# Stick-breaking attention: softplus, its parts and the log two steps ahead of the running total, scores three, and every second rounding on ScalarE

## The chip, the core and the metric

The kernel runs on one core of a Trainium2 chip. The core has five engines, each with its own instruction queue, worked off in order: TensorE (PE in the rows, PEld for its weight loads), VectorE (DVE), ScalarE (ACT), GpSimd (POOL) and SyncE (SP, which only starts transfers). The metric is the device time of one launch in microseconds (us). A difference under 0.3% (4.85 us of 1615.97) can't be told from no change.

## The reference, cut to what matters

One layer: a projection, gating and stick-breaking attention, an output projection, and a mixture of experts. The change is in the attention alone, 4 heads over 1024 positions:

```
z = einsum('bhqd,bhkd->bhqk', qb, kf[:, :, :kl]) * scale
causal = arange(kl)[None, :] < q_pos[:, None]
log_fail = where(causal, log_sigmoid(-z), 0.0)            # -softplus(z)
within = einsum('bhqni,ij->bhqnj', log_fail, after_in_block)
blk = sum(log_fail, axis=-1)
later = cumsum(blk, axis=3, reverse=True) - blk
log_a = log_sigmoid(z) + (within + later[..., None])
a = where(causal, exp(log_a), 0.0)
outs.append(einsum('bhqk,bhkd->bhqd', a, vt[:, :, :kl]))
```

The sum over later keys is a running total: a key block can only be finished when all later blocks have been added.

## The kernel before, in words

Attention works on transposed tiles: 128 keys on the partitions, up to 512 queries (one half of the sequence) along the row. A `Chain` is one head of one half. Two chains, an even and an odd head, go side by side as a pair. A step is one key block of a pair, from the last block (`top`) down to block 0; the list `seq` holds all 24 steps. On the diagonal a step has fewer columns: both pairs of the first half have steps of 128, 256, 384 and 512 columns (steps 0 to 3 and 4 to 7), both of the second half 128, 256, 384 and five times 512 (steps 8 to 15 and 16 to 23).

For each chain and step: `z` makes the scores on PE (plain float32, two passes each, and a mask product on the diagonal). `e0`, `e1`, `e2` make log(1+exp(-|z|)) on ACT, in tile `e`. `sp` adds max(z,0) on DVE, which gives softplus; it is then split in two parts, `sh` (rounded to float32r, line 682) and the rest `sl` (POOL, line 683). `ls` makes log_sigmoid(z) on DVE. `tri` adds both parts into the running total `cum` in PSUM with two matmuls, `add` (DVE, line 702) adds the total to `ls`, `comp` completes the total for the next block, `exp` is on ACT and `av` multiplies with V into `yp`.

The order on every engine is the order of the program text (`manual_schedule`). The loop at line 784 goes over k; one pass is called turn k here. Turn k does `tri`, `add`, `comp` and `exp` of step k, `av` of step k-1 (for the first step of a pair one turn later), and beside them work for later steps. When a pair has ended, `fin0` to `fin5` normalise its output: fin0 in the turn after (four ACT functions), fin1 to fin3 one turn later (column sums on PE, a power on POOL at line 128, a broadcast on PE at line 736, a product on DVE at line 740), then fin4 on ACT and fin5 (tile `yl`, DVE). This happens three times inside the loop, in turns 5, 9 and 17; the last pair is finished in the next stage, the output projection, which starts with `wo` on ACT.

Tiles come from rings: z has 4 buffers, e 4, sp 2, sh 4, sl 4, ls 8, two per step.

Of the kernel before, what the change touches and what calls it, by code (L numbers as in the profile page):

```python
# [11 lines left out]
F32R = mybir.dt.float32r  # L12
I32 = mybir.dt.int32
AF = mybir.ActivationFunctionType
# [3 lines left out]
P = 128  # L18
# [40 lines left out]
def body(ctx, tc, A, out):  # L59
    nc = tc.nc  # L60
    V, G, T, SC, SY = nc.vector, nc.gpsimd, nc.tensor, nc.scalar, nc.sync
# [364 lines left out]
    def at(s, fn):  # L426
        todo.setdefault(s, []).append(fn)
# [192 lines left out]
    def wo_load(i):  # L620
        if i < 16:
            cg, b = i // 4, (i + 2) % 4
            wo_raw[i] = wr.tile([P, 2, 512], F32, name="wo")
            SY.dma_start(wo_raw[i], A["w_out"][cg, b])
# [8 lines left out]
    def ya_load(t):  # L633
        y = op.tile([P, DG], F32, name="yld")
        SY.dma_start(y, y_d[t * P:(t + 1) * P, :])
        return y

    with ExitStack() as c3:
        at_ = c3.enter_context(tc.tile_pool(name="at", bufs=4, reuse_waits="tile"))
# [3 lines left out]
        class Chain:  # L643
# [31 lines left out]
            def sp(self, j):  # L675
                z, e = self.k[j]
                q0 = self.q0(j)
                sp = at_.tile([P, 512], F32, name="sp", bufs=2)[:, q0:]
                sh = at_.tile([P, 512], F32R, name="sh")[:, q0:]
                sl = at_.tile([P, 512], F32R, name="sl")[:, q0:]  # L680
                V.scalar_tensor_tensor(sp, z, 0.0, e, op0=ALU.max, op1=ALU.add)  # L681
                V.tensor_copy(sh, sp)  # L682
                G.tensor_tensor(sl, sp, sh.bitcast(F32), op=ALU.subtract)  # L683
                self.k[j] += [sh, sl]

# [66 lines left out]
        with tc.manual_schedule():  # L752
            seq = []
            for half in range(2):
                for hp2 in range(2):
                    ch = [Chain(half, 2 * hp2), Chain(half, 2 * hp2 + 1)]
                    seq += [(ch, j) for j in range((half + 1) * HT - 1, -1, -1)]
            n = len(seq)

            def each(i, f):  # L760
                if 0 <= i < n:
                    ch, j = seq[i]
                    for c in ch:
                        f(c, j)

            for i in range(2):
                wo_load(i)
            G.dma_start(wgr, A["w_gr"])
            yas = {t: ya_load(t) for t in range(2)}

            def scores(i):
                for f in (Chain.e0, Chain.e1, Chain.e2):
                    each(i, f)

            def first(i):
                return 0 <= i < n and seq[i][1] == seq[i][0][0].top

            each(0, Chain.z)
            each(1, Chain.z)
            scores(0)  # L780
            each(0, Chain.sp)
            each(0, Chain.ls)
            scores(1)
            for k in range(n + 1):
                each(k, Chain.tri)
                each(k, Chain.add)
                each(k + 2, Chain.z)
                each(k, Chain.comp)
                if 0 < k and seq[k - 1][1] == 0:
                    for i in range(6):  # L790
                        for c in seq[k - 1][0]:
                            at(k + (0, 1, 1, 1, 2, 3)[i], getattr(c, f"fin{i}"))
                if first(k - 2):
                    each(k - 2, Chain.av)
                if not first(k - 1):
                    each(k - 1, Chain.av)
                each(k + 1, Chain.sp)
                each(k + 1, Chain.ls)
                each(k + 2, Chain.e0)
                each(k, Chain.exp)  # L800
                each(k + 2, Chain.e1)
                each(k + 2, Chain.e2)
                for f in todo.pop(k, []) if k < n else ():
                    f()
            fins = [f for k in sorted(todo) for f in todo[k]]
            todo.clear()
# [386 lines left out]
    def pool(name, bufs=1):  # L1193
        return ctx.enter_context(tc.tile_pool(name=name, bufs=bufs, reuse_waits="tile"))
# [11 lines left out]
    sl = pool("sl")  # L1206
# [313 lines left out]
```

## Time and profile before

| | |
|---|---|
| median of 3 runs | 1615.97 us (1611.76 to 1616.34) |
| the profiled execution | 1613.13 us, of which 1611.4 us span |
| mean granted TensorE clock | 0.976 |
| PE busy in the span | 1517.6 us (94%) |
| DVE, ACT, POOL busy | 1217.1, 948.1 and 311.5 us |
| attention | from 536 to 667 us of the span |

A busy share over the span hides the stage: attention is 8% of the span, and its DMA queues are nearly idle. What the change does can only be seen there, in what each engine waits for.

### The profile page before, as it was taken

Reading aid. Unit: us, or ns where it says so; the run is one execution under the profiler, and the core shown is the slowest. Engines: PE = TensorE matmul, PEld = TensorE weight load, DVE = VectorE, ACT = ScalarE, POOL = GpSimd, SP = SyncE. Lnnn points to the kernel's source line nnn. Section 1 sums busy time; section 2 is a strip of 40 time slices with the busy share of each in tenths; the row PEclk is TensorE's granted clock in tenths of the full one; section 3 lists DMA queues with packets and bytes.
Section 4 is the critical chain, followed back from the end, with each engine's and each line's share of the span. In section 5 each row is a group of like instructions: output and inputs, shape, how many; then the busy total and the mean of one; then the engine's idle time right before and its main releaser. Section 6 shows DMA issues by size and latency. Waiting matters only on the chain.

```text
span 1611.4 us, 21345 instructions
## 1 busy us (share of the span) xinstructions
PE 1517.6 (94%) x6818; PEld 1150.6 (71%) x6818; DVE 1217.1 (76%) x2220; ACT 948.1 (59%) x2016; POOL 311.5 (19%) x286
## 2 busy tenths in 40 slices
PE   4999998999999899899999869999989999999996
PEld 4788887788888666578878756666656666666664
DVE  5889675867777588768756768887868888888883
ACT  5442588755434677532223567777767777777771
POOL 2000132010011244320001222324221212211111
PEclk9899999999999999999999979999999999999998
DMA  9987477768776000468857558999999999999982
GB/s 379 357 311 250 154 257 282 258 237 315 275 271 230 1 1 1 139 225 299 291 189 281 210 211 324 349 369 346 388 341 366 359 363 369 366 362 357 357 300 33
DMA packets 94393, 433.94 MB, mean 269 GB/s; under 512 B 13072, under 2 KB 13184, under 8 KB 64192
## 3 DMA queue, kind: packets, MB, share of 16 engines
q1 hardware_dynamic: 82000, 377.54, 63.3%
q0 software_dynamic: 11984, 52.85, 11.2%
q10 hardware_dynamic: 288, 2.10, 0.3%
q8 instruction: 56, 0.92, 0.2%
q14 instruction: 65, 0.53, 0.1%
HBM read 399.89 MB, written 43.02 MB: 275 GB/s over the span
## 4 chain that ended last, share of the span: by engine, by line
PE 38%; DMA 35%; issue 14%; DVE 6%; ACT 3%; POOL 2%; POOLq 0%; SPq 0%; another core or an unknown queue 0%; DVEq 0%; ACTq 0%
DMA out<-y,idx 22%; PE acc L322 21%; PE acc L867 9%; DMA xg<-u_d,idx 7%; DMA wm<-in_w_mod 2%; DMA out<-xi 2%; DVE macc L182 1%; PE lg L913 1%; PE yp L719 1%; POOL sl L683 1%; PE z L655 1%; DVE sp L681 1%; DVE sh L682 1%; PE tr L906 1%; ACT junk L347 1%
## 5 line engine op out<-in xcount | busy, mean ns | idle before, releaser
L1282 DVE TENSOR_TENSOR wl<-wx,wh 128x1024 fp32r<-128x1024 f32 x256 | 309.6, 1219 | 13.9 <-ACT wh L1281 12.9
L1281 ACT ACTIVATE wh<-wx 128x1024 fp32r<-128x1024 f32 x256 | 273.7, 1071 | 46.5 <-PE gu L1291 36.8
L1314 PE MATMUL dn<-wx,actT 128*128 128x512 f32 x512 | 241.9, 596 | 5.8 <-DMA wx<-in_w_down 5.2
L1291 PE MATMUL gu<-wh,xh 128*128 128x512 f32 x512 | 239.9, 469 | 0.0
L182 DVE SCALAR_TENSOR_TENSOR macc<-wm,sc_c,macc 128x512 f32<-128x512 f32 x296 | 222.3, 751 | 11.4 <-DMA wm<-in_w_mod 3.3
L322 PE MATMUL acc<-wh,hh 128*128 128x512 f32 x640 | 209.9, 398 | 3.2 <-ACT hh L278 1.8
L322 PE MATMUL acc<-wl,hh 128*128 128x512 f32 x640 | 206.9, 394 | 2.8 <-DVE wl L307 2.5
L322 PE MATMUL acc<-wh,hl 128*128 128x512 f32 x640 | 205.8, 392 | 0.4 <-DVE hl L279 0.4
L1291 PE MATMUL gu<-wl,xh 128*128 128x512 f32 x512 | 203.1, 397 | 0.1
L1291 PE MATMUL gu<-wh,xl 128*128 128x512 f32 x512 | 202.0, 394 | 0.0
L1224 POOL DMA_INDIRECT out<-y,idx x52 | 94.8, 1823 | 458.7 <-DVE y L1315 452.6
L1315 DVE TENSOR_TENSOR y<-dn,gate 128x512 f32<-128x512 f32 x128 | 88.6, 692 | 111.1 <-PE dn L1314 110.2
L867 PE MATMUL acc<-wo,yh 128*128 128x512 f32 x512 | 170.4, 414 | 0.0
L1270 ACT ACTIVATE xh<-tp,b2c 128x128 fp32r<-128x128 f32 x512 | 146.7, 384 | 18.0 <-PE tp L1265 18.0
L1314 PEld LDWEIGHTS dn<-wx,actT 128*128 128x128 f32 x512 | 96.6, 190 | 81.6 <-issue 63.2
L1272 DVE SCALAR_TENSOR_TENSOR xl<-tp,b2c,xh 128x128 fp32r<-128x128 f32 x512 | 143.5, 344 | 3.7 <-ACT xh L1270 3.7
L322 PEld LDWEIGHTS acc<-wl,hh 128*128 128x128 f32 x640 | 120.9, 189 | 30.0 <-DVE wl L307 4.9
L322 PEld LDWEIGHTS acc<-wh,hl 128*128 128x128 f32 x640 | 120.9, 189 | 26.7 <-DVE hl L279 1.1
L322 PEld LDWEIGHTS acc<-wh,hh 128*128 128x128 f32 x640 | 119.6, 190 | 27.2 <-ACT hh L278 1.9
L307 DVE TENSOR_TENSOR wl<-w,wh 128x1024 fp32r<-128x1024 f32 x80 | 97.6, 1221 | 33.4 <-ACT wh L306 33.3
L306 ACT ACTIVATE wh<-w 128x1024 fp32r<-128x1024 f32 x80 | 83.0, 1053 | 63.9 <-PE acc L322 53.8
L1291 PEld LDWEIGHTS gu<-wl,xh 128*128 128x128 f32 x512 | 97.5, 190 | 30.5 <-issue 15.1
(246 smaller groups left out, 2315.8 us busy)
## 6 DMA issues: line engine op xcount, KB each, us to landing
wx<-in_w_gu SPq DMA_DIRECT2D x128, 1024.0 KB, 23.1
wm<-in_w_mod SPq DMA_DIRECT2D x160, 512.0 KB, 5.4
wx<-in_w_down SPq DMA_DIRECT2D x64, 1024.0 KB, 21.6
w<-in_w_in SPq DMA_DIRECT2D x80, 512.0 KB, 5.5
x<-in_w_mod SPq DMA_DIRECT2D x16, 1024.0 KB, 5.7
wo<-in_w_out SPq DMA_DIRECT2D x16, 512.0 KB, 4.9
xi<-in_x SPq DMA_DIRECT2D x24, 256.0 KB, 5.9
out<-xi SPq DMA_DIRECT2D x24, 256.0 KB, 4.1
```

Source lines behind the costliest of these rows:

```text
L182: V.scalar_tensor_tensor(self.acc, t[:, j, :], sc, self.acc, op0=ALU.mult, op1=ALU.add)
L307: V.tensor_tensor(wl, w, wh.bitcast(F32), op=ALU.subtract)
L322: T.matmul(accs[t], a, b, start=(first and j == 0 and n == 0), stop=(last and j == 1 and n == 2))
L867: T.matmul(acc, y[a][:, c, ts_], w[b][:, c % 2, :], start=(n_ == 0 and i == 0), stop=(n_ == 7 and i == 2))
L1224: return G.indirect_dma_start(out=out, out_offset=bass.IndirectOffsetOnAxis(ap=idx, axis=0), in_=y, in_offset=None, bounds_check=S - 1, oo ...
L1270: SC.activation(xh[:, j, :], self.p[:, j, :], AF.Identity, bias=b2c[:, b * 4 + j:b * 4 + j + 1])
L1272: V.scalar_tensor_tensor(xl[:, j, :], self.p[:, j, :], b2c[:, b * 4 + j:b * 4 + j + 1], xh[:, j, :].bitcast(F32), op0=ALU.add, op1=ALU.sub ...
L1281: SC.activation(self.wh[q], w, AF.Copy)
L1282: low = lambda: V.tensor_tensor(self.wl[q], w, self.wh[q].bitcast(F32), op=ALU.subtract)
L1291: T.matmul(self.gu, a[c // 4][:, c % 4, :], b[q][:, k, :], start=(c == 0 and i == 0), stop=(c == 15 and i == 2))
L1314: T.matmul(d, self.aT[:, f, :], self.wd[f][:, cs], start=(f == 0), stop=(f == 1))
L1315: V.tensor_tensor(self.y[:, cs], d, gate2[:, cs], op=ALU.mult)
```

## The change

Three things at once. `sp`, both parts and `ls` are made for step k+2 in turn k, not for step k+1. `z` and the score functions are made for step k+3, not k+2. And for the odd head of each pair ACT writes `sh` in place of DVE. `sh` and `sl` get two more buffers each; the other rings keep their size.

```diff
-                sh = at_.tile([P, 512], F32R, name="sh")[:, q0:]
-                sl = at_.tile([P, 512], F32R, name="sl")[:, q0:]
+                sh = at_.tile([P, 512], F32R, name="sh", bufs=6)[:, q0:]
+                sl = at_.tile([P, 512], F32R, name="sl", bufs=6)[:, q0:]
                 V.scalar_tensor_tensor(sp, z, 0.0, e, op0=ALU.max, op1=ALU.add)
-                V.tensor_copy(sh, sp)
+                if self.h % 2:
+                    SC.activation(sh, sp, AF.Copy)
+                else:
+                    V.tensor_copy(sh, sp)
                 G.tensor_tensor(sl, sp, sh.bitcast(F32), op=ALU.subtract)
...
-            each(0, Chain.z)
-            each(1, Chain.z)
-            scores(0)
-            each(0, Chain.sp)
-            each(0, Chain.ls)
-            scores(1)
+            for i in range(3):
+                each(i, Chain.z)
+                scores(i)
+                if i < 2:
+                    each(i, Chain.sp)
+                    each(i, Chain.ls)
             for k in range(n + 1):
                 each(k, Chain.tri)
                 each(k, Chain.add)
-                each(k + 2, Chain.z)
+                each(k + 3, Chain.z)
                 each(k, Chain.comp)
...
-                each(k + 1, Chain.sp)
-                each(k + 1, Chain.ls)
-                each(k + 2, Chain.e0)
+                each(k + 2, Chain.sp)
+                each(k + 2, Chain.ls)
+                each(k + 3, Chain.e0)
                 each(k, Chain.exp)
-                each(k + 2, Chain.e1)
-                each(k + 2, Chain.e2)
+                each(k + 3, Chain.e1)
+                each(k + 3, Chain.e2)
```

The change shifts the lines of the program by three from line 685 on: `exp` is L713 before and L716 after, `add` L702 and L705.

What ACT has in a row in the second half, where a pair's wide steps end and the next pair's first step (128 columns) enters. Before (e is the score functions, ls the exp):

```order
L664 ACTIVATE e<-z 128x512 x2
L713 ACTIVATE ls<-ls 128x512 x2
L669 ACTIVATE e<-e 128x512 x2
L673 ACTIVATE e<-e 128x512 x2
L664 ACTIVATE e<-z 128x128 x2
L713 ACTIVATE ls<-ls 128x512 x2
```

The same place after:

```order
L683 ACTIVATE sh<-sp 128x512
L664 ACTIVATE e<-z 128x512 x2
L716 ACTIVATE ls<-ls 128x512 x2
L669 ACTIVATE e<-e 128x512 x2
L673 ACTIVATE e<-e 128x512 x2
L683 ACTIVATE sh<-sp 128x512
L664 ACTIVATE e<-z 128x128 x2
L716 ACTIVATE ls<-ls 128x512 x2
```

One rounding per turn now stands ahead of the score functions, and behind the last of the turn before.

ACT where the first pair has ended (u and og are fin0). Before:

```order
L673 ACTIVATE e<-e 128x384 x2
L724 ACTIVATE u_5029<-yp 128x512
L726 ACTIVATE og<-u_5029 128x512
L724 ACTIVATE u_5033<-yp 128x512
L726 ACTIVATE og<-u_5033 128x512
L664 ACTIVATE e<-z 128x512 x2
L713 ACTIVATE ls<-ls 128x256 x2
```

After:

```order
L673 ACTIVATE e<-e 128x512 x2
L727 ACTIVATE u_5059<-yp 128x512
L729 ACTIVATE og<-u_5059 128x512
L727 ACTIVATE u_5063<-yp 128x512
L729 ACTIVATE og<-u_5063 128x512
L683 ACTIVATE sh<-sp 128x512
L664 ACTIVATE e<-z 128x128 x2
```

The rounding of step 7 (512 columns) stands behind all four functions of fin0.

DVE one turn later, where fin1 to fin3 are (rs and u). Before:

```order
L681 SCALAR_TENSOR_TENSOR sp<-z,e 128x384
L682 CAST sh<-sp 128x384
L689 SCALAR_TENSOR_TENSOR ls<-z,e 128x384 x2
L125 TENSOR_SCALAR rs<-yp 128x4 x2
L740 SCALAR_TENSOR_TENSOR u_5029<-u_5029,hcol,yp 128x512
L740 SCALAR_TENSOR_TENSOR u_5033<-u_5033,hcol,yp 128x512
L702 TENSOR_TENSOR ls<-ls,cum 128x384 x2
L681 SCALAR_TENSOR_TENSOR sp<-z,e 128x512
```

After:

```order
L681 SCALAR_TENSOR_TENSOR sp<-z,e 128x512
L692 SCALAR_TENSOR_TENSOR ls<-z,e 128x512 x2
L125 TENSOR_SCALAR rs<-yp 128x4 x2
L743 SCALAR_TENSOR_TENSOR u_5059<-u_5059,hcol,yp 128x512
L743 SCALAR_TENSOR_TENSOR u_5063<-u_5063,hcol,yp 128x512
L705 TENSOR_TENSOR ls<-ls,cum 128x384 x2
L681 SCALAR_TENSOR_TENSOR sp<-z,e 128x128
```

Ahead of fin1 to fin3 now stands the softplus of a step that is one later, so 512 columns wide in place of 384, and the odd head's cast is gone.

## Rows read from the trace of the kernel before

**Rows 1.** Windows: us, busy us (x instructions) per engine, granted clock, DMA share, GB/s

```profile
606.00:616.00 10.00, 9.06 (x33) 5.35 (x33) 9.47 (x16) 7.29 (x17) 4.30 (x4) 1.00 0.00 0
...
633.00:635.00 2.00, 2.00 (x11) 2.00 (x10) 0.86 (x2) 0.00 (x0) 0.00 (x0) 0.50 0.00 0
```

**Rows 2.** Timeline of a 512-column step: start, us, engine, line, names [idle before <-releaser]

```profile
603.19 0.68 DVE L681 SCALAR_TENSOR_TENSOR sp<-z,e 128x512 f32<-128x512 f32 x1
603.90 0.43 DVE L682 CAST sh<-sp 128x512 fp32r<-128x512 f32 x1
604.25 0.68 DVE L681 SCALAR_TENSOR_TENSOR sp<-z,e 128x512 f32<-128x512 f32 x1
604.50 1.27 POOL L683 TENSOR_TENSOR sl<-sp,sh 128x512 fp32r<-128x512 f32 x1 [3.58 <-DVE sh L682]
604.97 1.09 DVE L682 CAST sh<-sp 128x512 fp32r<-128x512 f32 x1
...
607.55 0.49 PE L698 MATMUL cum<-sl,tri_r 128*128 128x512 f32 x1 [0.94 <-POOL sl L683]
...
608.69 0.68 DVE L681 SCALAR_TENSOR_TENSOR sp<-z,e 128x512 f32<-128x512 f32 x1
```

**Rows 3.** Timeline of ACT at 512 columns, one function behind the other

```profile
596.22 1.14 ACT L744 ACTIVATE yh<-u 128x512 fp32r<-128x512 f32 x2
597.26 1.07 ACT L664 ACTIVATE e<-z 128x512 f32<-128x512 f32 x2
598.21 1.15 ACT L713 ACTIVATE ls<-ls 128x512 f32<-128x512 f32 x2
599.25 1.15 ACT L669 ACTIVATE e<-e 128x512 f32<-128x512 f32 x2
```

**Rows 4.** Timeline of ACT at 128 and 384 columns

```profile
548.73 0.43 ACT L664 ACTIVATE e<-z 128x128 f32<-128x128 f32 x2
549.05 0.93 ACT L713 ACTIVATE ls<-ls 128x384 f32<-128x384 f32 x2
549.88 0.50 ACT L669 ACTIVATE e<-e 128x128 f32<-128x128 f32 x2
550.28 0.50 ACT L673 ACTIVATE e<-e 128x128 f32<-128x128 f32 x2
```

**Rows 5.** Timeline of PE: comp, then av of two 512-column chains

```profile
614.80 0.39 PE L709 MATMUL cum<-sl,comp_r 128*128 128x512 f32 x1
615.03 1.88 PE L719 MATMUL yp<-ls,x 128*128 128x512 f32 x4
```

**Rows 6.** Timeline of turn 5, the first pair's end

```profile
560.50 0.58 ACT L724 ACTIVATE u<-yp 128x512 f32<-128x512 f32 x1
561.18 0.55 DVE L681 SCALAR_TENSOR_TENSOR sp<-z,e 128x384 f32<-128x384 f32 x1
562.04 0.55 DVE L681 SCALAR_TENSOR_TENSOR sp<-z,e 128x384 f32<-128x384 f32 x1
562.80 1.06 ACT L664 ACTIVATE e<-z 128x512 f32<-128x512 f32 x2
563.70 1.01 POOL L683 TENSOR_TENSOR sl<-sp,sh 128x384 fp32r<-128x384 f32 x1 [0.39 <-DVE sh L682]
569.61 0.69 DVE L681 SCALAR_TENSOR_TENSOR sp<-z,e 128x512 f32<-128x512 f32 x1
```

**Rows 7.** Timeline of DVE around turn 17, the third pair's end

```profile
626.96 0.55 DVE L681 SCALAR_TENSOR_TENSOR sp<-z,e 128x384 f32<-128x384 f32 x1
636.34 0.68 DVE L681 SCALAR_TENSOR_TENSOR sp<-z,e 128x512 f32<-128x512 f32 x1
```

**Rows 8.** Timeline: softplus of steps 2 and 23, and the last exp

```profile
544.19 0.56 DVE L681 SCALAR_TENSOR_TENSOR sp<-z,e 128x384 f32<-128x384 f32 x1
...
660.24 0.68 DVE L681 SCALAR_TENSOR_TENSOR sp<-z,e 128x512 f32<-128x512 f32 x1
...
665.87 0.63 ACT L713 ACTIVATE ls<-ls 128x512 f32<-128x512 f32 x1 [0.30 <-DVE ls L702]
```

## Prediction, made before the changed kernel ran

> **What bounds the kernel now.** The diff touches only the attention, so I read the windows of that stage first: at 512 columns DVE works 9.47 of 10 us, PE 9.06, ACT 7.29 and POOL 4.30 [rows 1]. By shares DVE looks full. The timeline shows instead that a loop sets the pace. From the softplus of one 512-column step to that of the next are 5.50 us [rows 2]: sp even, cast, sp odd (1.74 until the odd one ends), the odd cast, the odd rest on POOL, the last tri on PE (at 607.55), the odd add, and only then the next sp. Each link waits for the one before. Two things are to be seen in those rows. The odd cast takes 1.09 us where the even one takes 0.43; POOL's sl runs beside the odd one. And ACT isn't in the loop: it has its 512-column functions ready long before DVE asks.
>
> The change takes that loop apart, since tri of a step then uses parts that were made a turn earlier. The question is which loop closes next.
>
> **The change part by part.** *Removed:* the odd cast on DVE (1.09 us at 512 columns, 24 of 48 casts), and the wait of tri for POOL. *Added:* 24 roundings on ACT. No row shows this very function; the nearest is fin4's copy to the same type, two in 1.04 us, so 0.52 each at 512 columns [rows 3]. Bounds are 0.48 (half of e0's 0.95, rows 3) and 0.57 (fin4's own 1.14 for two).
>
> *Moved:* sp, sh, sl and ls by one step, z and the score functions by one step. Nothing in SP's queue moves, POOL's transfers stay at the stage's end. The z ring still holds four tiles, so z of step k+3 waits for ls of step k+1, which is now done one turn earlier; that costs nothing while PE has slack.
>
> *Added waits:* ACT's rounding of the odd head waits for the odd sp on DVE. Queued behind it on ACT are the scores of the next step, the exp, and what DVE needs to start its next sp. That is a new loop: sp even, cast, sp odd (DVE), rounding, e0 pair, exp pair, e1 pair, first e2 (ACT), next sp even. At 512 columns: 1.74 [rows 2] + 0.52 + 0.95 + 1.04 + 1.04 + 0.63 [rows 3] (the single function is 1.15 less 0.52) + 0.06 for two hand-overs (estimate) = 5.97 us. It is longer than today's 5.50.
>
> One rule of the Trainium skill speaks to this place ("Perfetto Trace Analysis", Tensor Engine Instruction (MATMUL, LD_WEIGHTS)): ACT, DVE and GPSIMD take their instructions strictly first in, first out. By that the new loop stands; were later functions able to pass the rounding, the step would fall to PE's work. ACT's rows, where nothing overtakes, bear it out.
>
> For other widths I split a turn k in three: R for step k+2 (DVE part, rounding, hand-overs), X for step k (exp pair), Q for step k+3 (e0 pair, e1 pair, first e2).
> R: 2.32 at 512; at 384 0.86 + 0.55 [rows 6] + 0.41 + 0.06 = 1.88; 0.44 less per 128 columns, so 1.44 and 1.00 (estimates).
> X: 1.04 at 512, 0.83 at 384 and 0.40 at 128 [rows 3, 4], 0.61 between.
> Q: 2.62 at 512, 0.32 + 0.40 + 0.30 = 1.02 at 128 [rows 4], 1.55 and 2.08 between.
> Turns 0 to 4: 4.9 + 3.95 + 3.4 + 4.55 + 4.9 = 21.7. Turns 6 to 8: 3.4 + 4.55 + 4.9 = 12.85. Turns 10 to 16: 5.8 + 6.0 + 6.0 + 4.4 + 3.6 + 4.55 + 4.9 = 35.2. Turns 18 to 20: 5.8 + 6.0 + 6.0 = 17.8. Together 87.5 (87.4 unrounded).
> PE's own work is a second bound: a rounded product at 512 columns takes 0.23, a plain one 0.43 to 0.47 [rows 5], so a full turn has 8 x 0.23 + 8 x 0.43 = 5.3, under 5.97. It is longer than the ACT loop where a narrow step enters behind wide ones: in turn 14 PE has 0.94 (tri) + 1.0 (z and masks at 256) + 0.94 (comp) + 1.7 (av) = 4.6 against 3.6. PE has about half of that in hand, so 0.5; three others (turns 1, 2, 6) cost 0.4 together, and fin4 on ACT 0.1. Bounds: 0 and 1.9; I take 1.0. Ordinary turns: 88.4.
>
> Before, softplus of step 2 to that of step 23 takes 660.24 - 544.19 = 116.05 [rows 8], in which the three pair ends take 8.43, 8.98 and 9.38 (first and last in rows 6 and 7). The other 18 turns take 89.26. So **ordinary turns: -0.9 us**. The narrow ones gain, since their latency is covered; the 512-column ones lose 0.47 each, but for those where yl stood in DVE's way before.
>
> *Pair ends.* In turns 5, 9 and 17 everything waits for fin: POOL's power comes behind the odd sl, PE's broadcast behind the power, DVE's product behind that, and the next add and sp behind the product. Neither loop covers it, since DVE, ACT and PE all stop there in order. Before, the sl that POOL must finish first ends 3.53 us after the turn's sp even (563.70 + 1.01 - 561.18, rows 6), and the next sp comes 4.90 later, up to 5.9 in the last one. After, the softplus of that turn is 512 columns wide, and its odd rounding stands on ACT behind fin0's four functions, 2.30 us (560.50 to 562.80, rows 6). First e2 ends with the turn's start; its second takes 0.42 more; then 2.30; so the rounding starts at 2.72 where the odd sp alone would let it start at 1.77. It ends at 3.34, POOL starts 0.1 later (estimate) and needs 1.27 [rows 2]: 4.72. What follows is the same. **Pair ends: 3 x (4.72 - 3.53) = +3.6 us.** Bounds: without the hold of fin0 3 x 0.25 = 0.7; with a longer PE idle that drops the clock also at the first end, 4.6: in 633 to 635 the granted clock is 0.50, the 1.2 GHz level [rows 1], and the third end, where that is, took 0.95 longer than the first [rows 6, 7].
>
> *Start and end.* Three steps are prepared one behind the other before the first turn, and two narrow roundings (0.2 and 0.3 by the halves of rows 4) stand between them on ACT, in part in waits that are there anyway: **+0.2 us** (bounds 0 and 0.5). At the end the look-ahead has to be worked off: after the last sp even come, before, 5.63 us to the last exp's start and 0.63 for it, 6.26 [rows 8]. After, sp of step 23 is made one turn earlier, and two adds remain: sp and ls 3.0, add of step 22 1.3, its comp 0.5, av of step 21 1.7, tri of step 23 0.95, and add and exp of step 23 some 1.7: 9.1. **+2.8 us** (bounds +1.1, if PE has run ahead of av, and +3.5). Behind this exp ACT starts on `wo`; the loads that it waits for later are released by that `wo`, so they move along.
>
> Sum: -0.9 + 3.6 + 0.2 + 2.8 = +5.7 us, on the profiled execution's 1613.13: 1618.8. That execution is 2.84 under the median of the runs shown; the median plus 5.7 is 1621.7. I give 1619.5, near the first. 0.3% of 1615.97 is 4.85 us, about what a measurement of this kernel can tell from no change; the forecast is just above it.
>
> **The rivals.**
> *A, faster: the new loop doesn't close.* Then a turn takes what the busiest engine has, PE's 5.3 at 512 columns, and PE's work over the 18 ordinary turns is some 74 us by rows 5: 89.3 - 74 = 15 saved, less 3.6 + 0.2 + 2.8, so about -9: 1604. For it speaks that DVE is 95% busy [rows 1] and loses 1.09 per step. Against it: the same way of adding gives today's 5.5 from today's links, and ACT's rounding can't come before the odd sp. It decides from the point where the odd sp is ready before ACT is through with e2, 1.3 us earlier than I find it. The Trainium skill has the rule that would send it this way ("Perfetto Trace Analysis", Optimizing Scalar/DVE Operations): if DVE is saturated, work moved to Scalar may pay. By the rows DVE is busy but waits in a loop.
> *B, same: the pair ends don't grow,* because the fin chain is held by PE's column sums and not by POOL's sl. Then 0.7 in place of 3.6: +2.8, 1616. For it: fin1 needs the same fin0, and both are near each other in time; against it, POOL's order has sl ahead of the power. The same result comes if two steps of narrow width are cheaper than my estimates by 0.2 in each of 18 turns.
> *C, slower still:* PE waits longer before each broadcast, the clock falls to 1.2 GHz in all three ends and in the last turns, where PE is in the chain: +1 and +1.5 more, 1621 to 1623.
> That nothing changes, since another stage's transfer holds the end, I rule out nearly: the queues are idle there (DMA share 0.00, rows 1).
>
> **How the numbers follow.** Forecast (+4.9 to +7.5) 0.42, A 0.06, B and what lies between 0 and +4.8 0.38, C 0.14. Likeliest: 1619.5, its own range 1617 to 1622. Range of 8 in 10: 1613 (B on a run like the profiled one) to 1625 (C on a run like the median). Faster by over 0.3% 0.06, within 0.38, slower 0.56.
>
> **What would show it.** In the profile after: 512-column turns of about 6.0 us between two even sp; ACT idle some 1.3 us before each rounding, released by sp on DVE; PE no longer waiting for sl in ordinary turns (0.94 in rows 2); casts of 0.43 only; pair ends of 9.6 to 10.6 us, with the rounding behind fin0; some 9 us from the last even sp to the end of the last exp. I am wrong if 512-column turns come at 5.3 to 5.5, or if the pair ends take 8.4 to 9.4 as before.

## The result, and the profile after

The changed kernel takes 1628.21 us (median of 4 runs, 1626.84 to 1630.61), beside 1616.15 for the kernel before in runs on the same chip: a ratio of 1.0088 (95% interval 1.007 to 1.0105, written [1.007, 1.0105] from here on), slower by more than can be mistaken for no change. The forecast had the direction (slower, with a chance of 0.56) but 1619.5 us, and its range ended at 1625. Of the profiled executions, 1627.93 us stands against 1613.13, and their spans are 1626.1 and 1611.4 us.

Windows of the changed kernel: a stretch of 512-column turns, and the first pair end (columns as in [rows 1]):

```profile
611.00:617.00 6.00, 5.74 (x19) 3.13 (x18) 5.96 (x9) 5.01 (x10) 2.52 (x2) 1.00 0.00 0
570.00:577.00 7.00, 6.33 (x30) 6.25 (x31) 2.41 (x6) 3.32 (x11) 4.25 (x4) 0.52 0.00 0
```

In the second row PE looks busy, 6.33 of 7 us, but its granted clock is 0.52, nearly all at 1.2 GHz.

Timeline of one 512-column turn (answers to [rows 2]):

```profile
615.98 0.69 DVE L681 SCALAR_TENSOR_TENSOR sp<-z,e 128x512 f32<-128x512 f32 x1
616.70 0.43 DVE L685 CAST sh<-sp 128x512 fp32r<-128x512 f32 x1
617.04 0.68 DVE L681 SCALAR_TENSOR_TENSOR sp<-z,e 128x512 f32<-128x512 f32 x1
...
617.82 0.63 ACT L683 ACTIVATE sh<-sp 128x512 fp32r<-128x512 f32 x1 [1.43 <-DVE sp L681]
618.36 1.07 ACT L664 ACTIVATE e<-z 128x512 f32<-128x512 f32 x2
619.32 1.15 ACT L716 ACTIVATE ls<-ls 128x512 f32<-128x512 f32 x2
620.36 1.14 ACT L669 ACTIVATE e<-e 128x512 f32<-128x512 f32 x2
621.40 1.14 ACT L673 ACTIVATE e<-e 128x512 f32<-128x512 f32 x2
622.12 0.69 DVE L681 SCALAR_TENSOR_TENSOR sp<-z,e 128x512 f32<-128x512 f32 x1 [1.82 <-ACT e L673]
```

This is the loop of the forecast, link by link: ACT's rounding waits 1.43 us for the odd sp, and the next sp waits 1.82 for ACT's last function (`e2`). It takes 6.14 us, where 5.97 was forecast; in the kernel before the turn took 5.50 [rows 2]. The waits of the whole stage name the same two (us in total, times, longest), and the groups by line show what was added on ACT and what is left of the casts on DVE (24, mean 0.36 us):

```profile
ACT sh L683 <- DVE sp L681: 26.3, 19, 5.7
DVE sp L681 <- ACT e L673: 22.5, 15, 2.4
```

```profile
L683 ACT ACTIVATE sh<-sp 128x512 fp32r<-128x512 f32 (+3 forms) x24 | 12.5, 522 | 39.1 <-DVE sp L681 26.3 <-PE cum L712 6.7 <-PE z L655 6.1
L685 DVE CAST sh<-sp 128x512 fp32r<-128x512 f32 (+3 forms) x24 | 8.6, 360 | 0.8
```

Timeline of turn 5, the first pair end (answers to [rows 6]):

```profile
566.67 0.28 PE L712 MATMUL cum<-sl,comp_r 128*128 128x256 f32 x1
...
568.39 0.69 DVE L681 SCALAR_TENSOR_TENSOR sp<-z,e 128x512 f32<-128x512 f32 x1 [2.00 <-ACT e L673]
...
569.32 0.63 ACT L729 ACTIVATE og<-u 128x512 f32<-128x512 f32 x1
...
570.00 3.35 PE L733 MATMUL yp<-cst,og 128*128 128x1 f32 x16 [3.06 <-ACT og L729]
...
571.01 0.61 ACT L683 ACTIVATE sh<-sp 128x512 fp32r<-128x512 f32 x1
...
571.70 1.28 POOL L686 TENSOR_TENSOR sl<-sp,sh 128x512 fp32r<-128x512 f32 x1 [0.71 <-ACT sh L683]
...
572.93 2.02 POOL L128 TENSOR_TENSOR rs<-rs,mhalf 128x4 f32<-128x4 f32 x2
...
574.02 3.51 PE L739 MATMUL yp<-cst,rs 128*128 128x128 f32 x16 [0.67 <-POOL rs L128]
...
577.65 0.75 DVE L743 SCALAR_TENSOR_TENSOR u<-u,hcol,yp 128x512 f32<-128x512 f32 x1 [0.77 <-PE yp L739]
...
579.24 0.28 DVE L681 SCALAR_TENSOR_TENSOR sp<-z,e 128x128 f32<-128x128 f32 x1
```

PE stood idle for 3.06 us ahead of the column sums, and the broadcast took 3.51 us. In the kernel before the same groups of 16 products took 1.84 and 2.15 us, with no idle ahead of the column sums:

```profile
562.97 1.84 PE L730 MATMUL yp<-cst,og 128*128 128x1 f32 x16
...
565.75 2.15 PE L736 MATMUL yp<-cst,rs 128*128 128x128 f32 x16 [0.94 <-POOL rs L128]
```

The end of the attention, from the last even sp to the last exp (answers to [rows 8]): 9.09 us, in which DVE waits 3.00 for PE, and ACT in turn 3.06 for DVE.

```profile
669.57 0.69 DVE L681 SCALAR_TENSOR_TENSOR sp<-z,e 128x512 f32<-128x512 f32 x1 [2.15 <-ACT e L673]
...
676.71 1.28 DVE L705 TENSOR_TENSOR ls<-ls,cum 128x512 f32<-128x512 f32 x2 [3.00 <-PE cum L701]
...
677.43 1.23 ACT L716 ACTIVATE ls<-ls 128x512 f32<-128x512 f32 x2 [3.06 <-DVE ls L705]
```

From the first sp to the last exp the attention takes 141.6 us, 128.2 before. Cut at the even sp of each step, as in the forecast:

| part | before | after | change | forecast |
|---|---|---|---|---|
| start, step 0 to 2 | 5.86 | 6.28 | +0.4 | +0.2 |
| 18 ordinary turns | 89.26 | 93.48 | +4.2 | -0.9 |
| three pair ends | 26.79 | 32.76 (10.85, 11.16, 10.75) | +6.0 | +3.6 |
| end | 6.26 | 9.09 | +2.8 | +2.8 |
| together | 128.2 | 141.6 | +13.4 | +5.7 |

What is left of the 14.7 us between the two spans lies outside: the stage began 1.3 us earlier and what follows took 2.5 longer, both in stages that the change doesn't touch. In the profiles of all twelve kernels of this document the stage begins at 535.0 to 540.8 us and what follows takes 943 to 947, and the kernel that differs from the changed one in turn 1 alone has the shortest rest, 943.1; so a difference of this size outside the stage needs no cause in the attention. The medians differ by 12.

### The profile page after: what moved, and what is told of

Same layout as the page of the kernel before. It is cut to its first block, busy times and chain, and to the rows that moved or that the text cites. A ratio compares the mean times of both kernels' runs of the same rounds, so it can differ in the third digit from the quotient of the medians.

```text
span 1626.1 us, 21276 instructions
## 1 busy us (share of the span) xinstructions
PE 1521.8 (94%) x6818; PEld 1155.5 (71%) x6818; DVE 1198.0 (74%) x2196; ACT 957.2 (59%) x2040; POOL 312.5 (19%) x286
## 4 chain that ended last, share of the span: by engine, by line
PE 35%; DMA 34%; issue 15%; ACT 7%; DVE 6%; POOL 1%; POOLq 0%; SPq 0%; another core or an unknown queue 0%; DVEq 0%; ACTq 0%
DMA out<-y,idx 22%; PE acc L322 20%; PE acc L870 9%; DMA xg<-u_d,idx 7%; DMA wm<-in_w_mod 2%; DMA out<-xi 2%; PE lg L916 1%; DVE sp L681 1%; DVE macc L182 1%; ACT junk L347 1%; ACT qs L352 1%; ACT e L669 1%; PE tr L909 1%; ACT e L664 1%; PE yp L739 1%
## 5 line engine op out<-in xcount | busy, mean ns | idle before, releaser
L322 PEld LDWEIGHTS acc<-wl,hh 128*128 128x128 f32 x640 | 120.5, 189 | 30.3 <-DVE wl L307 5.4
```

What stands on the lines that cost most here:

```text
L322: T.matmul(accs[t], a, b, start=(first and j == 0 and n == 0), stop=(last and j == 1 and n == 2))
```

## The experiments

The two theories at the start. *Loop and clock:* the new loop costs what was forecast, and what came on top is PE's work at 1.2 GHz behind idle stretches that the look-ahead opens. *Rounding:* the odd rounding on ACT is the whole loss, by the loop and by its place behind fin0. All ratios below are to the kernel before in the same set of runs; turn lengths are from one profiled execution of each kernel. Ratios within 0.3% of 1 count as no change, also where the interval leaves 1 out.

**One part alone: the look-ahead, with both casts on DVE.**

```diff
-                if self.h % 2:
-                    SC.activation(sh, sp, AF.Copy)
-                else:
-                    V.tensor_copy(sh, sp)
+                V.tensor_copy(sh, sp)
```

> The look-ahead of the change alone; DVE rounds both heads, as before. Theory (the loop through ACT's rounding paces the turns, and PE's idle time in it brings the clock down): without the rounding on ACT no loop closes, a 512-column turn takes what DVE has to do, 5.3 to 5.4 us; pair ends some 0.8 us longer than before each (512 columns ahead of POOL's power), end +3. Sum by turns about 1612 to 1617, ratio to before 0.997 to 1.002. Rival (the look-ahead itself costs: later order at the pair ends, more to work off at the end): about as slow as the changed kernel, 1.006 to 1.009.

Measured: 1616.8 us, ratio 1.0009 [0.9999, 1.0018], no change. The 18 ordinary turns take 83.4 us, 5.9 less than before; a 512-column turn takes 5.20, and in it no wait is left on DVE:

```profile
599.26 0.68 DVE L681 SCALAR_TENSOR_TENSOR sp<-z,e 128x512 f32<-128x512 f32 x1
599.98 0.43 DVE L682 CAST sh<-sp 128x512 fp32r<-128x512 f32 x1
600.33 0.68 DVE L681 SCALAR_TENSOR_TENSOR sp<-z,e 128x512 f32<-128x512 f32 x1
601.04 1.10 DVE L682 CAST sh<-sp 128x512 fp32r<-128x512 f32 x1
602.07 1.27 DVE L689 SCALAR_TENSOR_TENSOR ls<-z,e 128x512 f32<-128x512 f32 x2
603.26 1.27 DVE L702 TENSOR_TENSOR ls<-ls,cum 128x512 f32<-128x512 f32 x2
604.46 0.68 DVE L681 SCALAR_TENSOR_TENSOR sp<-z,e 128x512 f32<-128x512 f32 x1
```

So the look-ahead does open the old loop. It gives the gain back at the pair ends (10.85, 10.89 and 10.18, +5.1 together, where 0.8 each was expected) and at the end (10.2, +3.9). With no rounding on ACT at all, turn 5 again has PE idle, here 1.49 us ahead of the broadcast, and a slow broadcast:

```profile
565.52 0.68 DVE L681 SCALAR_TENSOR_TENSOR sp<-z,e 128x512 f32<-128x512 f32 x1
...
568.56 1.27 POOL L683 TENSOR_TENSOR sl<-sp,sh 128x512 fp32r<-128x512 f32 x1 [0.46 <-DVE sh L682]
...
570.87 3.78 PE L736 MATMUL yp<-cst,rs 128*128 128x128 f32 x16 [1.49 <-POOL rs L128]
```

The odd sl ends 4.31 us after the turn's sp, against 4.59 in the changed kernel. So against a cast on DVE (1.09 us here too, beside POOL) the rounding behind fin0, which the forecast made the main cost of a pair end, makes 0.3 us. The pair ends grow without any rounding on ACT: for them it isn't the whole loss.

**The other part alone: the kernel before, with the odd rounding on ACT.** The edit is the one above in the other direction.

> The kernel before with only the rounding of the odd head moved to ACT, no look-ahead. Theory: the rounding stands ahead of the scores on ACT here too, so 512-column turns come at 6.0 to 6.15 us in place of 5.5; pair ends 0.8 us longer each; no extra at the end. Ratio to before 1.002 to 1.007. Rival (the look-ahead costs, the rounding relieves DVE): equal to before or faster, 0.995 to 1.000.

Measured: 1622.58 us, ratio 1.005 [1.0033, 1.0068]. The 512-column turns take 6.14, the same loop, without any look-ahead: it is the rounding's. The pair ends take 10.70, 10.68 and 10.68. DVE's busy time in the stage falls from 109 to 91 us while the stage grows by 8.7. Here too the broadcast at a pair end takes 3.78. The two parts don't add up: each alone lengthens the pair ends by more than 5 us, both together by 6.0, while in the ordinary turns the look-ahead alone gains 5.9, the rounding alone loses 3.1 and both lose 4.2.

**PE kept busy in turn 2.** In turn 1 of the changed kernel the scores of step 4 were made two times more for each head, and overwritten:

```diff
+        again = {(0, 1, 3): 2}
...
+                for _ in range(again.get((self.half, h // 2, j), 0)):
+                    T.matmul(zt, kT[:, h, j * P:(j + 1) * P],
+                             qT[:, h, self.half * HALF:(self.half + 1) * HALF], start=True,
+                             stop=True, skip_group_check=True)
```

> The changed kernel with four additional 512-column score products of two PE passes each (3.4 us of PE) in turn 1, ahead of z of step 4, which overwrites them; they fill the idle time of PE after which the granted clock fell to 0.50 in turn 2. Theory (clock): turn 2 falls from 6.2 us to about 3.6, no half clock there; the whole 2 to 3 us faster than the changed kernel, if no other stretch takes the fall over. Rival (turn 2 is long for a ring or a wait, not for the clock): turn 2 stays at 6 us or grows.

Measured: 1627.58 us, ratio 1.0082 [1.0065, 1.0099]. Turn 2 falls from 6.22 to 3.66, as expected, but the total doesn't follow: turn 6 takes 4.62 for 3.78, the pair ends 11.2, 11.09 and 11.09, the end 10.7. Turn 2 by itself proves less than it seems, as the runs below show.

**The odd rounding behind the scores.** ACT's rounding and POOL's rest of the odd head were put behind the scores of the same turn (a method of their own, `low`; ring of sp 4), so that ACT no longer waits for sp in the middle of the turn:

```diff
                 if self.h % 2:
-                    SC.activation(sh, sp, AF.Copy)
+                    self.late = (sp, sh, sl)
...
                 each(k + 3, Chain.e2)
                 for f in todo.pop(k, []) if k < n else ():
                     f()
+                each(k + 2, Chain.low)
```

> The changed kernel with ACT's rounding and POOL's rest of the odd head behind the scores and behind fin of the same turn (sp ring of 4 in place of 2). Theory (loop): ACT no longer waits for the odd sp, 512-column turns fall to PE's or DVE's work, 5.3 to 5.5 us; at the pair ends POOL's power comes ahead of the odd rest, 7.5 to 9 us each. Together some 20 us under the changed kernel: 1603 to 1611, ratio to before 0.992 to 0.997. Rival (what costs is the rounding's own time on ACT, or the look-ahead): within 5 us of the changed kernel.

Measured: 1615.53 us, ratio 1.0007 [0.9994, 1.002], no change. The loop is gone: the 512-column turns take 4.3 to 6.3 in place of 6.15. The expectation for the pair ends (7.5 to 9) failed outright: 11.55 to 11.75, DVE waiting 4.5 us for the broadcast in turn 5. Beside the changed kernel 13.6 us are gained in the ordinary turns, and the pair ends lose 2.3.

**PE kept busy at the three pair ends.** The edit of turn 2, applied in turns 5, 9 and 17 of the changed kernel instead.

> The changed kernel, and in each of the three pair-end turns PE repeats the score products of that turn twice for each head (four full 512-column products, overwritten by the real ones); nothing else. It tells apart why the three pair ends took 10.85, 11.16 and 10.75 us where 9.6, 10.2 and 10.6 were forecast. Theory (clock): in turn 5 of the changed kernel PE stood idle 3.06 us ahead of the column sums, the granted clock fell, and the broadcast took 3.32 us where it took 1.96 before; all else up to the odd sl came as forecast. With PE busy up to the column sums the broadcast takes about 2.0 again and turn 5 about 9.5; the three ends together lose 3 to 4 us, and the kernel comes to 1624 to 1626. Rival (the falls move): the number of falls stays, as when turn 2 was filled, and the time stays at 1626 to 1629. Rival (PE is not in the chain of the pair end, POOL and ACT are): turn lengths unchanged within 0.3 even where the broadcast is fast.

Measured: 1628.12 us, ratio 1.0087 [1.007, 1.0103]. The ends take 11.19, 10.48 and 9.45, with the broadcast at 3.78, 3.18 and 2.14. Turn 17, where the clock stayed up:

```profile
637.71 0.69 DVE L688 SCALAR_TENSOR_TENSOR sp<-z,e 128x512 f32<-128x512 f32 x1 [1.76 <-ACT e L680]
...
640.87 1.84 PE L740 MATMUL yp<-cst,og 128*128 128x1 f32 x16
641.02 1.27 POOL L693 TENSOR_TENSOR sl<-sp,sh 128x512 fp32r<-128x512 f32 x1 [0.71 <-ACT sh L690]
643.31 2.14 PE L746 MATMUL yp<-cst,rs 128*128 128x128 f32 x16 [0.60 <-POOL rs L128]
...
647.16 0.68 DVE L688 SCALAR_TENSOR_TENSOR sp<-z,e 128x512 f32<-128x512 f32 x1
```

The odd sl ends 4.58 after sp, and 4.87 later comes the next sp: the forecast's 4.72 and, for the first end, 4.90. With the clock up, the pair end is what was worked out. In the other two ends it fell all the same: the idle ahead of the broadcast was 1.80 and 0.97 us there, 0.60 in turn 17. The median of the total didn't move (the profiled execution, 1623.33, is the shortest of the six): keeping PE busy with idle work kept the clock up at one end of three and is no cure.

The same runs say more on turn 2, which this and the next kernel leave as it is. In the changed kernel PE waits there for DVE's ls, which frees the z buffers:

```profile
550.83 1.19 PE L655 MATMUL z<-xk 128*128 128x256 f32 x2 [3.23 <-DVE ls L692]
```

Windows of 3 us from the start of that z, in the changed kernel, in the one with busy pair ends, and in the next:

```profile
550.83:553.83 3.00, 3.00 (x9) 2.64 (x10) 2.09 (x6) 2.25 (x10) 1.94 (x4) 0.50 0.00 0
```

```profile
548.77:551.77 3.00, 3.00 (x10) 2.71 (x11) 2.10 (x6) 2.25 (x10) 1.95 (x4) 0.60 0.00 0
```

```profile
551.68:554.68 3.00, 3.00 (x17) 2.75 (x18) 2.58 (x8) 2.25 (x10) 1.95 (x4) 1.00 0.00 0
```

PE's idle ahead of that z was 3.23, 3.23 and 3.24 us. The turn took 6.22, 5.09 and 3.66. The same instructions behind the same idle stretch meet three mean clocks, and the turn's length follows the clock.

**fin2 and fin3 one turn later.** The broadcast behind tri of the turn after, the product behind its add, so that the next step's tri, add and sp no longer stand behind POOL's power:

```diff
             for k in range(n + 1):
                 each(k, Chain.tri)
+                for c in late.get(k, []):
+                    c.fin2()
                 each(k, Chain.add)
+                for c in late.get(k, []):
+                    c.fin3()
```

> The changed kernel, with fin2 (PE's broadcast) and fin3 (DVE's product) of each pair inside the loop one turn later: the broadcast behind tri, the product behind add, so that tri, add and softplus of the next step no longer stand behind POOL's power. Theory (the pair end's cost is that wait): the pair-end turns fall from 10.9 to 7 to 8 us, the turn behind each grows by 1.5 to 2, so 1.5 to 2.5 are gained at each end and the kernel comes to 1621 to 1624. Rival (the cost lies ahead of it, in fin0 on ACT and the column sums): the three pairs of turns keep their sum within 1 us, 1627 to 1629.

Measured: 1624.8 us, ratio 1.0062 [1.0046, 1.0077]. The pair ends changed little (10.88, 10.32, 10.17) where 7 to 8 were expected; the turns behind them hardly grew. Of the 3.4 us by which the stage got shorter, 2.6 are turn 2, whose clock stayed up. In turn 5 the broadcast now comes right behind tri, with no idle, and still takes 3.62 us; PE works without a gap from the column sums on, which wait 3.05 for fin0 as in the changed kernel. So the wait for the power is not the main cost here.

> The version with the odd rounding and its rest on POOL behind the scores, and fin2 and fin3 one turn later as well. There the pair ends took 11.6 to 11.75 us, with DVE 4.5 us in wait for the broadcast. Theory: that wait goes; each end with the turn behind it loses 3 to 5 us, the 512-column turns stay at 4.3 to 6.3, and the kernel comes to 1602 to 1608, faster than both kernels. Rival (the wait comes back as a wait of av or of the next sp, or as more time at half clock): 1611 to 1616.

Measured, both edits together: 1612.46 us, ratio 0.9981 [0.997, 0.9991], 3 less than with the late rounding alone. The ends stayed at 10.76, 10.74 and 10.21, because POOL's power still stood behind two rests that were late (568.37, behind the rounding, and 569.34; the power at 570.57, in turn 5).

> The kernel before, with fin2 and fin3 one turn later. Theory: in the kernel before too the pair end is a wait for power and broadcast (DVE 1.87 us, PE 1.03), not of the look-ahead's making; the pair ends fall from 8.4 to 9.4 to about 6.5, the turn behind grows by 1.5: 1 us or so saved at each, 1611 to 1614. Rival: without look-ahead add and sp wait for tri and POOL anyway and nothing is saved, 1615 to 1617.

Measured, the same edit on the kernel before: 1610.75 us, ratio 0.9979 [0.9968, 0.999]. Its ends fall from 8.43, 8.98 and 9.38 to 7.49, 7.46 and 7.45, all three with the same length, and the mean granted clock from sp of step 0 to the last exp is 1.00, where it was 0.97.

**fin3 behind the next softplus.** fin2 behind comp and fin3 behind the next sp pair; in the late-rounding version the rounding also goes ahead of fin0.

```diff
                 each(k, Chain.comp)
+                for c in late.get(k, []):
+                    c.fin2()
...
+                each(k + 1, Chain.sp)
+                for c in late.get(k, []):
+                    c.fin3()
                 if first(k - 2):
                     each(k - 2, Chain.av)
```

> As the late-rounding version with fin2 and fin3 one turn later, with two places moved: the odd rounding and its rest ahead of fin0 and fin1 (POOL's power then no longer waits behind a rest that is late), and in the later turn fin2 behind comp and fin3 behind the next softplus pair, so that no add and no softplus waits for the broadcast. Theory: the turns of 10.76, 10.74 and 10.21 fall to 6 to 8 us, with 1 to 1.5 on the turn behind for av, which waits for fin3; 6 to 9 us less than that version, 1603 to 1607. Rival: the power is late for the column sums alone and av's wait grows by what the softplus loses: 1610 to 1613.

Measured: 1611.67 us, ratio 0.9988 [0.9978, 0.9998]: the rival. The ends fall to 6.51, 6.07 and 5.89, and the turns behind them grow from 4.3 to 8.92, from 5.6 to 9.33 and from 4.7 to 10.76; all 21 turns together take 110.6 us, 110.9 in the version before. The wait has moved on: in turn 6 DVE waits 3.43 us for the broadcast ahead of its product, with the granted clock at 0.80.

> The kernel before, with fin2 one turn later behind comp and fin3 behind the next softplus pair. With fin2 behind tri and fin3 behind add the pair-end turns took 7.46, DVE waiting 0.61 and 0.32 for the broadcast and the softplus behind it. Theory: they fall to 5.5 to 6, and av's wait adds 0.5 to 1 on the turn behind: 1607 to 1610. Rival: PE's idle ahead of av drops the clock and takes it back: 1610 to 1612.

Measured: 1608.11 us, ratio 0.9965 [0.9951, 0.9978]: the lowest median of all, and faster than both kernels (its interval overlaps that of the version before, 0.9979). Its ends take 5.05, the turns behind them 7.3 to 7.5 (5.5 before): 6 us less in sum, with a mean granted clock of 1.00 in the stage. In turn 6 DVE makes the products without a wait, and PE waits 1.06 for them:

```profile
570.57 1.39 DVE L740 SCALAR_TENSOR_TENSOR u<-u,hcol,yp 128x512 f32<-128x512 f32 x2
```

```profile
568.36 1.95 PE L736 MATMUL yp<-cst,rs 128*128 128x128 f32 x16
571.36 0.49 PE L719 MATMUL yp<-ls,x 128*128 128x128 f32 x2 [1.06 <-DVE u L740]
```

## Why the prediction was right in its direction and wrong in its size

**The old loop and the new one: right.** The look-ahead takes the old loop apart (5.50 to 5.20 alone), and the rounding closes a longer one, with or without look-ahead. Rival A didn't come. The rule of the Trainium skill ("Perfetto Trace Analysis", Optimizing Scalar/DVE Operations) that would have sent it that way needs a saturated DVE; the rounding alone took 18 us of busy time off DVE and made the kernel 0.5% slower, so DVE was busy but not the bound.

**The loop's length: 5.97 forecast, 6.14 measured.** (The forecast's terms add up to 5.98.) The term that was mis-sized is "0.06 for two hand-overs". The rows show 0.10 from the odd sp's end (617.72) to the rounding and 0.09 from the first e2's end (621.40 + 0.63) to sp; the rounding itself costs 0.54. Most of the 17 ordinary turns other than turn 2 came 0.1 to 0.2 over their loop estimates, turns 14, 6 and 20 by 0.3, 0.4 and 0.5. They sum to 87.3 where 85.0 was forecast (88.4, with 1.0 for PE in it, less turn 2's 3.4): +2.3.

**The clock: the step that failed.** Of a pair end the forecast said "What follows is the same." Up to the odd sl it held: 4.59, 4.57 and 4.57 where 4.72 was forecast. Behind it came 6.26, 6.59 and 6.18 in place of 4.90, 5.45 and 5.85. The broadcast in these took 3.51, 3.78 and 3.44, mostly at the lower clock, where in the kernel before it took 2.15, 2.65 and 3.06 (there too the clock was lower at the second and third end, 0.78 and 0.65 over the broadcast). In all six, and in turn 17 with a busy PE (2.14, and 4.87 in all), what follows the odd sl is the broadcast and 2.7 to 2.8 us more: it grew by what the broadcast grew, 2.9 in sum. Less the 0.13 to 0.15 by which each first part came in under, that is +2.4 in all. Turn 2 took 6.22 where 3.4 was forecast, +2.8, of which the clock is 2.6: without the fall it took 3.66. The mean granted clock of the stage was 0.92, 0.97 before. Rival C named this mechanism, but it saw it at the broadcasts and in the last turns only, at +2.5, and gave it 0.14.

The miss in the stage is then 2.3 + 2.4 + 2.8 + 0.2 (start) = 7.7 of the 13.4 - 5.7.

**Where PE's idle comes from.** The forecast counted what moved on DVE, ACT and POOL, and PE only as a bound on length; of the wait of z for ls it said "that costs nothing while PE has slack". PE's largest wait in the stage before, and two of those after (us in total, times, longest):

```profile
PE cum L698 <- POOL sl L683: 9.8, 17, 0.9
```

```profile
PE z L655 <- DVE ls L692: 6.9, 5, 3.2
PE yp L733 <- ACT og L729: 6.9, 3, 3.1
```

Many short waits for sl have become a few long ones. PE no longer waits for sl, runs ahead, and then stands still at what the new loop delivers: the ls that frees the z buffers (turn 2), and fin0's og (the pair ends). In turn 5 PE was through with comp at 566.95 and the first og came at 569.95; before, og was there at 561.74 and PE busy until 562.97. Of that idle, 1.0 us is PE's own shorter work (3.29 us from the first tri to the column sums before, 2.26 after), since z was 128 columns wide in place of 512; the rest is fin0, which stands on ACT behind score functions that the rounding holds up. In the look-ahead alone the first og comes 2.60 us after the turn's first tri, where it is 5.27 in the changed kernel and 2.06 in the one before; there PE has only 0.48 us of idle ahead of the column sums, and 1.49 ahead of the broadcast, behind the wider softplus. In the rounding alone the idle ahead of the broadcast is 1.09 in turn 5. So either part by itself leaves PE idle at the pair ends, each in another place. That the wait in turn 2 would go with a larger z ring is not shown.

**The end: right**, 9.09 for 9.1, in part by luck: single terms missed by up to 0.4 (av took 1.3 for 1.7) and cancelled. **Rival B** (pair ends don't grow) didn't come.

**Open:** why the clock falls at one such place and not at the next with the same idle. In the kernel before, PE's idle ahead of the broadcast was 0.94, 0.92 and 0.92 us at the three ends, and the broadcasts ran at 1.00, 0.78 and 0.65. So it is shown that the lower clock lengthens the chain, but that longer idle stretches bring it down is argued and not shown. Runs with PE kept busy didn't lower the total, so what the falls cost in all is not measured; shown is what they cost at the places named.

## What to carry to other kernels

Before moving work earlier, list for every engine what it was filling there, and what it will meet once it runs ahead: PE's short waits became a few long idle stretches, the clock fell behind some of them, and the products that followed in the chain took up to 1.8 times as long. Handing a link of a loop to another engine with work queued behind it didn't relieve the busy engine here; it changed the loop's members and made it longer. The stall worth removing stood in the profile before, at the pair ends: a product put behind work that didn't need it gave 0.35% with no look-ahead at all.

## What was not expected of the hardware

The same idle of 3.23 to 3.24 us ahead of the same products was followed by a granted clock of 0.50, 0.60 and 1.00 over 3 us in three runs, so one profile can't say what such a place costs. At the lower clock the 16 broadcast products took 3.8 us for 2.15, and the 16 column-sum products 3.35 for 1.84.

The odd cast's 1.09 us [rows 2] is no property of the odd head. With the odd rounding behind the scores, POOL's odd rest runs beside the even cast, and that one grows. Timeline of that kernel (POOL and the even casts of two turns):

```profile
609.17 1.29 POOL L693 TENSOR_TENSOR sl<-sp,sh 128x512 fp32r<-128x512 f32 x1 [2.07 <-ACT sh L692]
...
610.08 0.66 DVE L685 CAST sh<-sp 128x512 fp32r<-128x512 f32 x1
...
613.78 1.29 POOL L693 TENSOR_TENSOR sl<-sp,sh 128x512 fp32r<-128x512 f32 x1 [1.58 <-ACT sh L692]
...
614.38 0.97 DVE L685 CAST sh<-sp 128x512 fp32r<-128x512 f32 x1
```

Both casts end 0.28 us after POOL's instruction does (610.74 and 610.46, 615.35 and 615.07); the odd cast of the kernel before ends 0.29 after it (606.06 and 605.77) [rows 2]. In these three a cast that starts while POOL subtracts lasts until POOL is through. The Trainium skill says the same of the port pair that both use ("SBUF — State Buffer", SBUF: two separate sides): whoever is first has it for the whole instruction. So the 1.09 of the forecast's first term was mostly a wait. In the stage before, the 48 casts took 30.3 us, and the 24 that stayed on DVE took 8.6: of the 21.7 us that seemed to be the odd casts' work, some 13 (estimate, by 0.36 a cast) were this wait, and DVE's 95% held it too.
